# Down projections of a decoder block as seven-product quads in the pipeline of gate and up

## The chip, the cores and the metric

One core of a Trainium2 chip runs the whole block as one program. The metric is the device time of one execution in microseconds (us). TensorE (PE, with its weight loads PEld), VectorE (DVE), ScalarE (ACT), GpSimd (POOL) and SyncE (SP, which issues the transfers) work side by side, each through its own instructions in a fixed order.

## What is computed

The input is x, 2048 tokens by 1024 features, all in float32.

```python
xn = rmsnorm(h, g_mix); z = xn @ w_in + b_in           # 1024 -> 1536
y_conv = silu(layernorm(causal_depthwise_conv(a * sigmoid(gate))))   # 512 features, 31 taps
y_pool = (trailing mean over 2, 4, 8 or 16 tokens minus the token) @ w_pool * s_pool
h = h + concat(y_conv, y_pool) @ w_out
h = h + (silu(n @ w_gate) * (n @ w_up)) @ w_down        # n = rmsnorm(h, g_ffn); 1024 -> 2816 -> 1024
out = rmsnorm(h, g_final)
```

## The kernel before

The tokens are cut into two superblocks of 1024 (`a0`, `a1`), and each superblock into two halves of 512 tokens, which is the width of a matmul. Features lie on the partitions in blocks of 128. A product in float32 is made of three matmuls: every operand is split into a high and a low part (`split`, lines 195 and 196: ScalarE casts the high part, VectorE subtracts it to get the low part), and `mm3` (lines 204 to 206) adds high by high, high by low and low by high. So each operand that comes from memory costs a cast and a subtraction before TensorE can use it.

The order of the work, in the words of the program's end (from `a0, a1 = Sup(0), Sup(1)`): the input projection of superblock 0, then that of superblock 1 with superblock 0's convolution on VectorE beside it. Then for superblock 0 the output projection and `turn` (the norm and the start of gate and up), gate and up, and the down projection; then the same for superblock 1. Superblock 1's pooling and convolution (`bg`, some 160 steps, most of them one VectorE operation of 128x1024 in line 491) are spread by `beside` over superblock 0's gate and up, one step for each yield, and over its first two down groups.

**Gate and up** use seven products in place of eight (Strassen's scheme in a form that chains sums in PSUM). A `Quad` makes two output blocks for two halves of tokens from two blocks of weights. Its seven factors of the activations (`self.t`, made by `put_t`) stay in SBUF for the whole stage. Its weights are loaded two quads ahead (`load`, lines 851 and 852), summed (`sums`, lines 864 to 867) and split. `product` writes the banks of a two-bank accumulator (`quad`) and of one bank of `chain`; ScalarE copies banks on (lines 911, 916, 918), and VectorE and ScalarE form the results (lines 879 to 884). The seventh product's result is read from the accumulator's second bank before the third product adds to that bank. A gate quad and an up quad share one tile `at`, which is stored to `at_d`.

**Down** runs in three groups of 8, 8 and 6 blocks of the 22 (`GROUPS`). `down_load` (line 738) loads and splits the group's activations, `down` makes for each of eight output blocks a plain product into `pd`, and line 761 adds it to h, which is loaded from and stored to `h_d` (lines 756 and 765). The last group of superblock 1 is `down_last`.

Storage is given out by an `Arena`: 17 units for staging (`arena`), 36 for split operands (`arena_r`). `take` gives, in program order, the units that have been free longest; a tile of 1 MB takes two units. What the next user of a unit does must wait until the one before has been read. The order in which each engine runs its instructions is then set by a scheduler that keeps to dependences and prefers what comes first in the program.

## Time and profile before

| | |
|---|---|
| median of 3 runs (lowest to highest) | 1903.79 us (1899.77 to 1904.42) |
| profiled execution, its own time | 1902.86 us |
| span of its trace | 1901.1 us |
| mean granted TensorE clock | 0.987 |
| busy: PE, DVE, ACT | 97%, 65%, 33% |
| matmuls in the trace | 7995 |
| transfers | 263.96 MB, mean 139 GB/s |

"Busy" is the time in which an engine had an instruction in it, as a share of the span. A matmul is listed with 0.39 us, but the next starts before it ends, so that the distance between starts, not the listed length, says how many fit in a stretch. The granted clock is that of TensorE: 1.00 is 2.4 GHz, 0.50 is 1.2 GHz. An idle time in brackets behind an instruction is what its engine waited before it, and what ended the wait.

### The profile page before, as it was taken

Reading aid. Unit: us, or ns where it says so; the run is one execution under the profiler, and the core shown is the slowest. Engines: PE = TensorE matmul, PEld = TensorE weight load, DVE = VectorE, ACT = ScalarE, POOL = GpSimd, SP = SyncE. Lnnn points to the kernel's source line nnn. Section 1 sums busy time; section 2 is a strip of 40 time slices with the busy share of each in tenths; the row PEclk is TensorE's granted clock in tenths of the full one; section 3 lists DMA queues with packets and bytes.
Section 4 is the critical chain, followed back from the end, with each engine's and each line's share of the span. In section 5 each row is a group of like instructions: output and inputs, shape, how many; then the busy total and the mean of one; then the engine's idle time right before and its main releaser. Section 6 shows DMA issues by size and latency. Waiting matters only on the chain.

```text
span 1901.1 us, 19811 instructions
## 1 busy us (share of the span) xinstructions
PE 1841.0 (97%) x7995; PEld 1497.5 (79%) x7995; DVE 1234.7 (65%) x1359; ACT 623.2 (33%) x796; POOL 51.4 (3%) x41
## 2 busy tenths in 40 slices
PE   8999999998999999998999999899999999999996
PEld 6777887876788888877788888678888888888885
DVE  4989997488997999992542546866554545523235
ACT  5255124244333333341221323433333333412110
POOL 0103200000000000000000000000000000000000
PEclk9999999999999999998999999899999999999998
DMA  7263125523422232143583753155131113635422
GB/s 284 75 212 123 67 90 172 205 78 122 167 79 88 73 116 78 67 188 133 190 313 130 285 199 111 47 198 199 45 132 67 67 67 147 252 144 215 154 85 89
DMA packets 70235, 263.96 MB, mean 139 GB/s; under 512 B 7168, under 2 KB 11392, under 8 KB 56320
## 3 DMA queue, kind: packets, MB, share of 16 engines
q1 hardware_dynamic: 68848, 260.52, 38.1%
q10 hardware_dynamic: 1296, 2.19, 0.3%
q8 instruction: 62, 1.02, 0.2%
q14 instruction: 29, 0.24, 0.0%
HBM read 189.19 MB, written 73.49 MB: 138 GB/s over the span
## 4 chain that ended last, share of the span: by engine, by line
PE 83%; DVE 8%; DMA 4%; ACT 1%; issue 1%; POOL 0%; POOLq 0%; DVEq 0%; SPq 0%; ACTq 0%
PE pd L206 8%; PE pd L204 8%; PE pd L205 8%; PE quad L204 8%; PE quad L206 8%; PE quad L205 8%; PE chain L204 6%; PE chain L205 6%; PE chain L206 6%; PE px L204 3%; PE px L205 3%; PE px L206 3%; DVE arena_r L196 2%; DVE arena L491 2%; PE pa L206 1%
## 5 line engine op out<-in xcount | busy, mean ns | idle before, releaser
L195 ACT CAST arena_r<-arena 128x1024 fp32r<-128x1024 f32 (+3 forms) x375 | 364.4, 984 | 848.1 <-PE pd L205 228.9
L196 DVE TENSOR_TENSOR arena_r<-arena,arena_r 128x1024 fp32r<-128x1024 f32 (+3 forms) x375 | 422.2, 1138 | 246.5 <-ACT arena_r L195 215.5
L491 DVE SCALAR_TENSOR_TENSOR arena<-arena,par_sb 128x1024 f32<-128x1024 f32 (+1 forms) x240 | 287.2, 1212 | 2.3
L204 PE MATMUL quad<-arena_r 128*128 128x512 f32 x704 | 276.2, 393 | 11.7 <-ACT arena_r L195 10.8
L204 PE MATMUL pd<-arena_r 128*128 128x512 f32 x704 | 276.1, 392 | 9.9 <-ACT arena_r L195 9.1
L205 PE MATMUL quad<-arena_r 128*128 128x512 f32 x704 | 276.2, 392 | 0.8 <-DVE arena_r L196 0.8
L206 PE MATMUL pd<-arena_r 128*128 128x512 f32 x704 | 275.1, 391 | 1.8 <-DVE arena_r L196 1.8
L206 PE MATMUL quad<-arena_r 128*128 128x512 f32 x704 | 275.8, 392 | 0.0
L205 PE MATMUL pd<-arena_r 128*128 128x512 f32 x704 | 274.6, 390 | 0.0
L204 PE MATMUL chain<-arena_r 128*128 128x512 f32 x528 | 212.1, 402 | 4.9 <-ACT arena L916 2.8
L205 PE MATMUL chain<-arena_r 128*128 128x512 f32 x528 | 207.1, 392 | 0.9 <-DVE arena_r L196 0.9
L206 PE MATMUL chain<-arena_r 128*128 128x512 f32 x528 | 207.1, 392 | 0.0
L761 DVE TENSOR_TENSOR arena<-pd,arena 128x1024 f32<-128x1024 f32 x40 | 48.9, 1223 | 187.8 <-PE pd L206 186.7
L204 PEld LDWEIGHTS quad<-arena_r 128*128 128x128 f32 x704 | 133.3, 190 | 41.7 <-ACT arena_r L195 12.1
L204 PEld LDWEIGHTS pd<-arena_r 128*128 128x128 f32 x704 | 132.7, 188 | 39.1 <-ACT arena_r L195 10.2
L206 PEld LDWEIGHTS pd<-arena_r 128*128 128x128 f32 x704 | 132.5, 188 | 31.4 <-DVE arena_r L196 4.0
L205 PEld LDWEIGHTS quad<-arena_r 128*128 128x128 f32 x704 | 133.2, 189 | 29.3 <-DVE arena_r L196 1.9
L206 PEld LDWEIGHTS quad<-arena_r 128*128 128x128 f32 x704 | 133.3, 189 | 28.2 <-DVE arena_r L196 0.4
L205 PEld LDWEIGHTS pd<-arena_r 128*128 128x128 f32 x704 | 132.6, 188 | 27.9 <-issue 0.5
L204 PEld LDWEIGHTS chain<-arena_r 128*128 128x128 f32 x528 | 99.6, 189 | 38.0 <-ACT chain L911 8.8
L205 PEld LDWEIGHTS chain<-arena_r 128*128 128x128 f32 x528 | 99.9, 189 | 21.8 <-DVE arena_r L196 2.2
L206 PEld LDWEIGHTS chain<-arena_r 128*128 128x128 f32 x528 | 99.7, 189 | 21.8
(135 smaller groups left out, 2082.8 us busy)
## 6 DMA issues: line engine op xcount, KB each, us to landing
arena<-h_d SPq DMA_DIRECT2D x28, 1024.0 KB, 5.6
arena<-in_wg SPq DMA_DIRECT2D x44, 512.0 KB, 5.1
arena<-in_wu SPq DMA_DIRECT2D x44, 512.0 KB, 5.1
at_d<-arena SPq DMA_DIRECT2D x22, 1024.0 KB, 4.4
arena<-at_d SPq DMA_DIRECT2D x22, 1024.0 KB, 5.7
h_d<-arena SPq DMA_DIRECT2D x20, 1024.0 KB, 4.3
arena<-in_wd SPq DMA_DIRECT2D x32, 512.0 KB, 4.4
arena<-in_x SPq DMA_DIRECT2D x12, 1024.0 KB, 6.4
```

Source lines behind the costliest of these rows:

```text
L195: nc.scalar.copy(hi, y)
L196: tt(out=lo, in0=y, in1=hi.bitcast(F32), op=ALU.subtract)
L204: nc.tensor.matmul(acc, lhsT=w[:, 0, c], rhs=hi, start=start, stop=False, **kw)
L205: nc.tensor.matmul(acc, lhsT=w[:, 0, c], rhs=lo, start=False, stop=False, **kw)
L206: nc.tensor.matmul(acc, lhsT=w[:, 1, c], rhs=hi, start=False, stop=stop, **kw)
L491: stt(out=v, in0=u.ap[:, j : j + n], scalar=w, in1=v, op0=ALU.mult, op1=ALU.add)
L761: tt(out=v, in0=acc, in1=v, op=ALU.add)
```

## The change

Groups 0 and 1 of the down projection become quads too (`DownQuad`, four for each group), behind the 22 gate and up quads in the same pipeline. Their seven factors are formed while up quads end (`close`: four more VectorE subtractions for each up quad, stored to `t_d`), and loaded and split by `factors`, one for each product of the last quad ahead of a group. The quad adds its results to h (`open` loads it, `close` stores it). Group 2 stays as it was, with its loads stepped beside the last down quad (`follow`). `beside` now spreads `bg` over all quads, six steps for seven yields in place of one for one. In `turn`, the second norm's row sums go to a bank of the first quad's accumulator (`s.bank`) and stand ahead of three of the first four products; at the front, `x_spread` stands ahead of the second input tile.

```diff
+    t_d = [[dr.tile([P, 7, 4, T], F32, name=f"t_d{s}_{g}", bufs=1) for g in range(STRASSEN)] for s in range(NS)]
...
 
-        def __init__(self, src, halves=False, parts=None):
+        def __init__(self, src, halves=False, parts=None, pairs=None):
+            self.place = (lambda k: (k % pairs, k // pairs)) if pairs else (lambda k: (k // 2, k % 2))
             n = src.shape[1] // 2 if parts is None else T
             st = Buf(arena, 2 * n)
             v = st.ap.rearrange("p (a n) -> p a n", a=2)
...
                 ww, c = self(k)
-                r = mov[k // 2].v
+                i, h = self.place(k)
+                r = mov[i].v
                 for b, acc in accs:
-                    mm3(acc, ww, c, (r[:, 0, k % 2, b], r[:, 1, k % 2, b]), n == 0, n == len(ks) - 1)
+                    mm3(acc, ww, c, (r[:, 0, h, b], r[:, 1, h, b]), n == 0, n == len(ks) - 1)
 
         def free(self):
             self.w.free()
...
             self.t = {}
-            at = None
-            quads = []
-            for n in range(2 * NFP):
-                quads.append(Quad(self, n))
+            quads = [Quad(self, n) for n in range(2 * NFP)]
+            self.td = [{} for _ in range(STRASSEN)]
+            for g in range(STRASSEN):
+                quads[-1].follow = self.factors(g)
+                quads += [DownQuad(self, g, q, len(quads) + q) for q in range(NQ)]
+            quads[-1].follow = self.follow = self.down_load(STRASSEN)
             q0, q1 = quads[:2]
             q0.load()
             q1.load()
...
             q1.sums()
-            yield
-            for q in (q0, q1):
-                q.product(1)
-                q.product(2)
+            q0.begin()
+            q1.begin()
+            self.bank = q0.acc[:, 1]
+            yield
+            q0.product(1)
+            yield
+            q0.product(2)
+            yield
+            q1.product(1)
+            q1.product(2)
             q1.mid()
             yield
             yield from self.put_t(5, *B11, B12, B11)
...
-            for n in range(2, 2 * NFP):
+            for n in range(2, len(quads) - 2):
...
                 cur.product(3)
                 yield
 
+        def factors(self, g):
+
+            for p, i in ((1, 0), (2, 2), (6, 5), (5, 1), (7, 4), (4, 6), (3, 3)):
+                t = B4("tl")
+                nc.sync.dma_start(t.ap, t_d[self.s][g][:, i].rearrange("p n t -> p (n t)"))
+                self.td[g][p] = r = R("td")
+                for j in range(2):
+                    split(r.v[:, 0, j], r.v[:, 1, j], t.v[:, j])
+                t.free()
+                yield
+
         def down_load(self, g):
-            a = []
+            self.a = a = []
             for fp in range(*GROUPS[g]):
                 t = B4("al")
                 nc.sync.dma_start(t.ap, at_d[self.s][fp])
...
+
+        def open(self):
+            if self.gate:
+                Quad.at = B4("at")
+            self.at = Quad.at
+            self.o = self.at.v
+
+        def close(self):
+            if self.gate:
+                return
+            g, j = divmod(self.fp, 4)
+            if g < STRASSEN:
+                o = self.o
+                tx = B4("tx")
+                for dst, i0, i1 in (
+                    (tx.v[:, 0, 0], o[:, 1, 1], o[:, 0, 1]),
+                    (o[:, 0, 1], o[:, 0, 1], o[:, 0, 0]),
+                    (tx.v[:, 0, 1], o[:, 1, 1], o[:, 0, 1]),
+                    (tx.v[:, 1, 0], o[:, 1, 0], tx.v[:, 0, 1]),
+                ):
+                    tt(out=dst, in0=i0, in1=i1, op=ALU.subtract)
+                nc.sync.dma_start(t_d[self.sup.s][g][:, :4, j], self.at.ap.rearrange("p (n t) -> p n t", n=4))
+                nc.sync.dma_start(t_d[self.sup.s][g][:, 4:, j], tx.ap[:, : 3 * T].rearrange("p (n t) -> p n t", n=3))
+                tx.free()
+            else:
+                nc.sync.dma_start(at_d[self.sup.s][self.fp], self.at.ap)
+            self.at.free()
...
+        def begin(self):
+            if self.acc is None:
+                self.acc = ps2("quad")
+
-                self.acc = ps2("quad")
-                if self.gate:
-                    Quad.at = B4("at")
-                self.at = Quad.at
-                self.o = self.at.v
+                self.begin()
+                self.open()
-            r = self.sup.t[p].v
+            r = self.t[p].v
...
-            if self.n == 2 * NFP - 1:
-                self.sup.t.pop(p).free()
+            if self.follow:
+                self.t.pop(p).free()
+                step(self.follow)
...
-                if not self.gate:
-                    nc.sync.dma_start(at_d[self.sup.s][self.fp], self.at.ap)
-                    self.at.free()
+                self.close()
+
+    class DownQuad(Quad):
+
+
+        def __init__(self, sup, g, q, n):
+            self.sup, self.q = sup, q
+            self.s1, self.s2 = wd[g][2 * q], wd[g][2 * q + 1]
+            self.w = {}
+            self.ch = chain_bank[n % 2]
+            self.t = sup.td[g]
+            self.follow = None
+
+        def open(self):
+            self.h = B4("h")
+            nc.sync.dma_start(self.h.ap, h_d[self.sup.s][self.q])
+
+        def close(self):
+            nc.sync.dma_start(h_d[self.sup.s][self.q], self.h.ap)
+            self.h.free()
+
+        def result(self, a, b, acc, extra=None):
+            dst = self.h.v[:, a, b]
+            if extra is not None:
+                tt(out=dst, in0=dst, in1=extra, op=ALU.add)
+            tt(out=dst, in0=acc, in1=dst, op=ALU.add)
...
     wb.free()
     run(sq)
-    pa1 = a0.in_tile(in0.get(), "pa")
+    w = in0.get()
     a0.x_spread()
+    pa1 = a0.in_tile(w, "pa")
     a0.in_evac(0, pa, pg)
     cv = a0.mix_branches()
     pg1 = a0.in_tile(in0.get(), "pg")
...
                 step(gu, 2)
             elif n == 6:
                 step(gu)
-        nm = s.norm(1, s.hr)
+        nm = s.norm(1, s.hr, s.bank)
         step(gu)
-        step(nm, 2)
+        step(nm)
         step(gu)
+        step(nm)
+        step(gu, 2)
         step(nm)
         step(gu, 2)
         step(nm)
...
     g0 = a0.gate_up()
     turn(a0, g0)
     bg = seq(a1.pools(), a1.mix_branches())
-    beside(g0, bg, 6, 6)
-    beside(a0.down(0, a0.down_load(0)), bg, 3, 1)
-    beside(a0.down(1, a0.down_load(1)), bg, 4, 1)
+    beside(g0, bg, 6, 7)
     run(bg)
-    dn = a0.down(2, a0.down_load(2))
+    run(a0.follow)
+    dn = a0.down(STRASSEN)
     step(dn, 2)
     run(a1.y_load((2, 3, 0, 1)))
     step(dn, 4)
...
-    for g in range(len(GROUPS) - 1):
-        run(a1.down(g, a1.down_load(g)))
-    run(a1.down_last(len(GROUPS) - 1, a1.down_load(len(GROUPS) - 1)))
+    run(a1.follow)
+    run(a1.down_last(len(GROUPS) - 1))
```

The order of the instructions moves in three places that matter. The first is ScalarE near the program's start. `arena<-chain` is the copy of the norm's spread that the first evacuation needs. Before:

```order
L390 ACTIVATE arena,xss<-arena 128x1024 x4
L195 CAST arena_r<-arena 128x1024 x2
L199 ACTIVATE arena_r<-arena,par_sb 128x128 x4
L195 CAST arena_r<-arena 128x1024 x2
L399 COPY arena<-chain 128x1024
```

In the changed kernel:

```order
L393 ACTIVATE arena,xss<-arena 128x1024 x4
L197 CAST arena_r<-arena 128x1024 x3
L201 ACTIVATE arena_r<-arena,par_sb 128x128
L402 COPY arena<-chain 128x1024
L201 ACTIVATE arena_r<-arena,par_sb 128x128 x3
L197 CAST arena_r<-arena 128x1024
```

The copy has moved ahead of a cast and of three scaled casts; on TensorE the matmul that it waits for now stands 46 matmuls earlier.

The second is VectorE in superblock 0's turn. `px` is the output projection, `rv` the row scales of the second norm, `rb` their spread, L884 (L938 in the changed kernel) the result of the first up quad's second product. Before:

```order
L615 TENSOR_TENSOR arena<-px,arena 128x512
L196 TENSOR_TENSOR arena_r<-arena,arena_r 128x1024
L299 TENSOR_TENSOR arena<-arena 128x512
L323 TENSOR_SCALAR rv<-pv 128x4
L330 CAST rs<-rr 128x4
L331 TENSOR_TENSOR rs<-rr,rs 128x4
L334 TENSOR_TENSOR arena_r<-ident,rs 128x512 x2
L884 TENSOR_TENSOR arena<-quad,arena 128x512
L634 SCALAR_TENSOR_TENSOR arena<-arena,par_sb,rb 128x512 x3
L647 TENSOR_TENSOR arena<-arena 128x2x512
```

In the changed kernel:

```order
L618 TENSOR_TENSOR arena<-px,arena 128x512
L303 TENSOR_TENSOR arena<-arena 128x512
L326 TENSOR_SCALAR rv<-quad 128x4
L333 CAST rs<-rr 128x4
L334 TENSOR_TENSOR rs<-rr,rs 128x4
L337 TENSOR_TENSOR arena_r<-ident,rs 128x512 x2
L637 SCALAR_TENSOR_TENSOR arena<-arena,par_sb,rb 128x512 x2
L198 TENSOR_TENSOR arena_r<-arena,arena_r 128x1024
L650 TENSOR_TENSOR arena<-arena 128x2x512
L637 SCALAR_TENSOR_TENSOR arena<-arena,par_sb,rb 128x512 x2
L198 TENSOR_TENSOR arena_r<-arena,arena_r 128x1024
L938 TENSOR_TENSOR arena<-quad,arena 128x512
```

The norm no longer stands behind the result of the up quad, which shows that the products it belongs to now come after the norm's row sums.

The third is VectorE where superblock 0's first group of the down projection ends. Before, this is `down` (L761 adds a finished product to h) with the layer norm (L546, L309) beside it:

```order
L761 TENSOR_TENSOR arena<-pd,arena 128x1024
L196 TENSOR_TENSOR arena_r<-arena,arena_r 128x1024
L761 TENSOR_TENSOR arena<-pd,arena 128x1024
L196 TENSOR_TENSOR arena_r<-arena,arena_r 128x1024 x3
L761 TENSOR_TENSOR arena<-pd,arena 128x1024
L546 TENSOR_TENSOR arena<-arena,mu 128x1024 x3
```

In the changed kernel it is the fourth down quad, with the splits of the second factor set (L198), convolution steps (L494) and weight sums (L891, L892) between its results (L1005, L1006):

```order
L1006 TENSOR_TENSOR arena<-quad,arena 128x512 x2
L494 SCALAR_TENSOR_TENSOR arena<-arena,par_sb 128x1024
L198 TENSOR_TENSOR arena_r<-arena,arena_r 128x1024 x3
L494 SCALAR_TENSOR_TENSOR arena<-arena,par_sb 128x1024
L198 TENSOR_TENSOR arena_r<-arena,arena_r 128x1024 x2
L198 TENSOR_TENSOR arena_r<-arena,arena_r 128x512
L494 SCALAR_TENSOR_TENSOR arena<-arena,par_sb 128x1024
L891 TENSOR_TENSOR arena<-arena 128x512
L1005 TENSOR_TENSOR arena<-arena 128x512
L892 TENSOR_TENSOR arena<-arena 128x512
L198 TENSOR_TENSOR arena_r<-arena,arena_r 128x1024 x2
```

Six convolution steps or so stand in each down quad, where before the convolution was over by the start of the down projection; the factor splits come on top of them.

## Rows read from the trace of the kernel before

**Rows 1.** The page: busy time by engine, and the chain of waits by engine.

```profile
PE 1841.0 (97%) x7995; PEld 1497.5 (79%) x7995; DVE 1234.7 (65%) x1359; ACT 623.2 (33%) x796; POOL 51.4 (3%) x41
...
PE 83%; DVE 8%; DMA 4%; ACT 1%; issue 1%; POOL 0%; POOLq 0%; DVEq 0%; SPq 0%; ACTq 0%
```

**Rows 2.** Stage windows: stretch and length; PE, PEld, DVE, ACT, POOL busy (count); clock, DMA, GB/s.

```profile
946.50:1110.00 163.50, 163.50 (x722) 135.23 (x721) 70.00 (x62) 44.48 (x45) 0.00 (x0) 1.00 0.67 244
1268.50:1635.00 366.50, 366.50 (x1607) 299.89 (x1606) 194.58 (x237) 133.04 (x178) 0.00 (x0) 1.00 0.31 114
```

**Rows 3.** Stage windows at superblock 0's change from gate and up to down.

```profile
851.00:856.00 5.00, 0.94 (x5) 0.44 (x3) 3.65 (x4) 1.99 (x2) 0.00 (x0) 0.89 0.41 156
856.00:861.00 5.00, 0.33 (x1) 0.33 (x2) 0.35 (x1) 1.04 (x1) 0.00 (x0) 0.50 0.86 261
861.00:866.00 5.00, 4.96 (x13) 3.42 (x13) 0.88 (x1) 0.43 (x1) 0.00 (x0) 0.59 0.57 213
```

**Rows 4.** Timeline of PE, superblock 0's down: start, length, instruction, [wait before it].

```profile
860.67 0.80 PE L204 MATMUL pd<-arena_r 128*128 128x512 f32 x1 [8.73 <-ACT arena_r L195]
...
919.84 0.50 PE L204 MATMUL pd<-arena_r 128*128 128x512 f32 x1 [0.41 <-ACT arena_r L195]
921.88 0.50 PE L206 MATMUL pd<-arena_r 128*128 128x512 f32 x1 [1.30 <-DVE arena_r L196]
```

**Rows 5.** Stage windows: gate and up of superblock 0, then of superblock 1.

```profile
451.00:832.00 381.00, 380.11 (x1665) 310.29 (x1664) 349.64 (x382) 133.07 (x182) 0.00 (x0) 1.00 0.29 103
1255.00:1636.00 381.00, 381.00 (x1677) 311.62 (x1675) 204.67 (x250) 138.40 (x185) 2.48 (x1) 1.00 0.32 116
```

**Rows 6.** Timeline of DVE in superblock 0's gate and up.

```profile
647.50 0.68 DVE L865 TENSOR_TENSOR arena<-arena 128x512 f32<-128x512 f32 x1
648.11 1.28 DVE L491 SCALAR_TENSOR_TENSOR arena<-arena,par_sb 128x1024 f32<-128x1024 f32 x1
649.30 0.68 DVE L866 TENSOR_TENSOR arena<-arena 128x512 f32<-128x512 f32 x1
...
842.27 3.49 DVE L196 TENSOR_TENSOR arena_r<-arena,arena_r 128x1024 fp32r<-128x1024 f32 x3
```

**Rows 7.** Timelines of SP, ACT and DVE: one load of the down projection's activations, split.

```profile
845.79 0.32 SPq L738 DMA_DIRECT2D arena<-at_d  x1
...
851.04 1.99 ACT L195 CAST arena_r<-arena 128x1024 fp32r<-128x1024 f32 x2 [4.89 <-DMA arena<-at_d]
...
853.31 2.35 DVE L196 TENSOR_TENSOR arena_r<-arena,arena_r 128x1024 fp32r<-128x1024 f32 x2
```

**Rows 8.** The page's DMA issues, then instructions of `at_d`, loads and stores together.

```profile
arena<-at_d SPq DMA_DIRECT2D x22, 1024.0 KB, 5.7
...
DMA to landing us min/median/max: 4.2/5.0/8.7
```

**Rows 9.** Groups by line and shape: busy us, mean ns of one, idle before.

```profile
L918 ACT COPY arena<-chain 128x512 f32<-128x512 f32 x44 | 25.9, 588 | 79.4 <-PE chain L206 79.4
```

**Rows 10.** Timelines of DVE and PE in superblock 0's turn, then a stage window.

```profile
417.73 0.68 DVE L299 TENSOR_TENSOR arena<-arena 128x512 f32<-128x512 f32 x1
...
421.26 0.95 PE L316 MATMUL pv<-ones,arena 128*128 128x1 f32 x8
...
430.20 1.22 PE L204 MATMUL quad<-arena_r 128*128 128x512 f32 x2 [4.49 <-ACT arena_r L195]
...
430.00:435.00 5.00, 4.64 (x10) 3.25 (x11) 5.00 (x6) 1.20 (x2) 0.00 (x0) 0.50 0.00 0
```

**Rows 11.** Timeline of PE at the front, then two stage windows.

```profile
48.35 0.40 PE L346 MATMUL chain<-arena_r,ones_r 128*128 128x512 f32 x1
...
51.91 0.47 PE L204 MATMUL pg<-arena_r 128*128 128x512 f32 x1 [3.16 <-DVE arena L411]
...
40.00:50.00 10.00, 8.75 (x39) 6.89 (x37) 0.60 (x1) 1.68 (x2) 0.17 (x1) 1.00 0.12 45
50.00:60.00 10.00, 8.09 (x29) 6.52 (x30) 9.86 (x9) 3.66 (x4) 0.21 (x1) 0.83 0.30 105
```

More of the change, by code (lines that the diff above doesn't have):

```diff
@@ L185, in block_kernel @@
     class W(Buf):
[L188 removed]
+        WHERE = (range(7 * RU, NR), range(NR))
         def __init__(self, units, n=T):
@@ L550, in ln @@
             yield
-            var.rows(1.0 / CC, LN_EPS, chain if first else None)
+            var.rows(1.0 / CC, LN_EPS, flat(chain) if first else None)
             yield
@@ L625, in mix_out, with norm @@
                     r.free()
-        def norm(self, b, hr):
-            hr.rows(1.0 / D, RMS_EPS)
+        def norm(self, b, hr, bank=None):
+            hr.rows(1.0 / D, RMS_EPS, bank)
             yield
@@ L742, in down_load, with down @@
                 t.free()
-            return a
-        def down(self, g, a):
+                yield
+            self.ws = Ahead([lambda m=m: Dense(wd[g][m], pairs=GROUPS[g][1] - GROUPS[g][0]) for m in range(KD)], 1)
+            self.ws.prime(2)
+            yield
+        def down(self, g):
+            a, ws = self.a, self.ws
             n = len(a)
@@ L749, in down @@
                 self.fr = Rms(whole=True)
-            ws = Ahead([lambda m=m: Dense(wd[g][m]) for m in range(KD)], 1)
-            ws.prime(2)
             for m in range(KD):
```

15 lines of the change are left out of this document (9 added, 6 removed).

## The prediction

> **What bounds the kernel now.** I read the busy times and the chain of waits first: TensorE is busy 97% of the span and carries 83% of the chain that ends last [rows 1]. So I counted matmuls. One is listed as lasting 0.39 us, but each starts before the one ahead has ended; its price is the interval. The stage windows give it: 721 weight loads in 163.5 us of down projection, 0.2268 us each, and 1606 in 366.5 us of gate and up, 0.2282 us each, both at full clock [rows 2]. Then I looked for places where TensorE runs short of that pace. Four matter here: the front, the change from output projection to gate and up ("turn") of each superblock, and, in superblock 0 alone, the change from gate and up to down. Last I read VectorE by stage. In superblock 0's gate and up, with the convolution of superblock 1 beside it, VectorE is busy 349.6 of 381 us (92%); in superblock 1's, 204.7 of 381 us (54%) [rows 5]. That difference decides most of what follows.
>
> **Matmuls removed.** Groups 0 and 1 of a superblock's down projection were 2 x 8 output tiles x 8 blocks x 2 halves x 3 passes = 768 matmuls. As eight quads of 7 products x 4 blocks x 3 passes they are 672. 768 x 0.2268 = 174.2 us; 672 x 0.2282 = 153.4 us; so 20.8 us less per superblock on the engine that sets the end.
>
> **Superblock 1.** Nothing runs beside it, and the order of instructions puts the factor loads and splits a quad (84 x 0.2282 = 19.2 us) ahead of their use. VectorE spends 1.14 us on a 1024-wide subtraction, 0.61 us on a 512-wide one and 1.20 us on a convolution step, by the distance between starts [rows 6]. A down quad gives it 3 wide and 11 narrow operations: 10.1 us. The 14 wide splits of a factor set add 16 us, spread over two quads, so no quad passes 19.2 us by much. I take 20 us; the ends are 21 (nothing waits) and 15 (two or three waits of 2 us for each factor set, like the small waits of [rows 4]).
>
> **Superblock 0, what leaves.** At the change to down, TensorE waits 8.73 us for the first weights and then runs at half clock, 0.50 and 0.59 of full [rows 3, 4]. In those 15 us it does 5+1+13 = 19 matmuls; at pace there would be 66, so 10.7 us are lost. Down quads now follow up quads in one pipeline, with weights fetched two quads ahead, so this goes. A later wait of 1.3 us at the layer norm and 0.4 us before it go as well. With the matmuls that is 20.8 + 10.7 + 1.7 = 33.2 us to be had.
>
> **Superblock 0, what comes.** First, VectorE. In the new order, from the last up quad's seventh product to the sixth down quad's, it has 46 wide subtractions, 67 narrow operations and 29 convolution steps: 52.4 + 40.9 + 34.8 = 128.1 us. TensorE needs six quads, 115.2 us, and about 1.9 us for four layer-norm matmuls: 117.1 us. VectorE falls 11 us behind. Its result of the seventh product must be read before the third product may write the same bank; two products (24 x 0.2282 = 5.5 us) lie between, less one copy on ScalarE (0.59 us [rows 9]) and two narrow operations (1.2 us). So 3.7 us are cover and 7.3 us become waiting.
>
> Second, the staging of factors. Working the arena's rule through in program order, five of the seven loads of the first set, and six of the second, take one and the same pair of units, since the convolution holds most others. Such a load can start only when the one before is split. The trace shows one such link: load issued at 845.79, two casts from 851.04, two subtractions from 853.31 [rows 7]. Priced apart: 5.7 us for 1 MB [rows 8], 2.0 us of casts, 1.2 us for the last subtraction, 8.9 us together. Counting from the end of the first product of the quad that steps the loads (the first load is in by then), the second set's five links finish at 3.2 + 5 x 8.9 = 47.7 us; its last factor is wanted 15 products later, at 15 x 12 x 0.2282 = 41.1 us. So it is 6.6 us late. The first set, with four links, is ready at 40.9 us, just in time. 7.3 + 6.6 = 13.9; I take 14 us. Ends: if loads land as fast as the quickest (4.2 us) and the reserve holds, 7; if as slowly as the slowest (8.7 us), the second chain is 3.0 x 5 = 15 us later and no cover is left for the 11 us, 33 us. A wait of ScalarE's cast for such a load also holds back the bank copies queued behind it, and TensorE waits for those; this lies within the same ends.
>
> For the load the trace has 4.2 to 8.7 us for 1 MB, with 5.7 in the median [rows 8], in company with weights. The Trainium skill (SBUF — State Buffer, "The DMA setup-cost knee") fits 2 us plus bytes over 436 GB/s, an estimate of 4.4 us here. By that the links would be 1.3 us shorter, the last factor 0.1 us late, and the sum 6.5 us better.
>
> So superblock 0 gives 33.2 - 14 = 19 us (0 to 26).
>
> **Turns.** The second norm's row sums now stand ahead of 24 first-pair products instead of behind them, in a bank of the quad's own accumulator. TensorE got to them at 421.26, while what they sum was ready at 417.73 + 0.68 = 418.4 [rows 10]. So the norm starts 2.9 us sooner, and the 24 moved products (5.5 us) cover the 4.49 us wait after it. I take 3 us per turn, 6 in all. At most the wait and the half-clock stretch go whole, 4.5 + 2.6 us each; at least nothing, as VectorE's chain of sums and splits behind it is no shorter. I use 0 to 11 for both.
>
> **Front.** The spread of x's norm is moved ahead of the second input tile. Its fourth matmul had stood behind that tile, at 48.35; the evacuation of the first pair followed, and the next tile waited 3.16 us for a bank and began at reduced clock [rows 11]. From 40 to 60 us there are 39 + 29 = 68 matmuls where 20 / 0.2268 = 88 fit: 4.6 us. All of it should go: the fourth needs nothing that the three ahead of the tile did not have. Ends 2 (a later wait takes some back) and 6.
>
> **Costed at nothing:** the four extra subtractions per up quad (2.4 us in 38.4) displace one convolution step in seven (one of seven yields per quad, 2.4 us per pair), so VectorE stays at about 92%; the extra stores and loads of factors, some 25 MB, fall on DMA engines that are busy 29 to 32% in those stages [rows 5]. If that cover went, they would show as late loads, priced above.
>
> **Sum.** 4.6 + 6 + 19 + 20 = 49.6 us off the profiled execution's 1902.9 us: 1853 us. The median of the runs shown is 0.9 us above that execution, which I leave out.
>
> **The rivals.** (a) The stalls are hidden: loads land like the quickest [rows 8], convolution steps slip behind the quads' own work, and less than 7 us of waiting is left in superblock 0. For it: most loads have a quad of slack. Against: one pair of units, and a VectorE that is full in every link. 1853 - 14 = 1839 us with none left, 1833 with the best ends of turns and front, 1842 in the middle. (b) VectorE and staging eat superblock 0's gain: stalls near 33 us, 19 us more than forecast, 1872 us. For it: in-order queues, where one late load stops results behind it. (c) Slower than before: every factor load of superblock 0 lands on the path, 14 x 8.9 = 125 us against 63.8 us (33.2 + 20 + 6 + 4.6) gained elsewhere, 1964 us. It decides from the eighth exposed load on. Against it: the first loads of each set find free units well ahead. (d) Stalls cancel the whole gain, near 1903 us: the same mechanism with seven loads exposed.
>
> **How the numbers follow.** Forecast 0.57 (1846 to 1862), (a) 0.19, (b) 0.17, (c) 0.04, (d) 0.03. About 0.3%, 6 us, can be told from no change. Faster 0.94, same 0.02, slower 0.04. The range, 1835 to 1875 us, holds the forecast, most of (a) and (b), and leaves out the rest.
>
> **What would show it.** Matmuls fewer by 192; no wait of 8 us near 850 us; 20 us less between superblock 1's last up quad and its third group; in superblock 0's down quads VectorE near full and TensorE waiting on results of the seventh product and on casts behind factor loads; the 3.16 us wait at 52 us gone. It is wrong if those quads run at TensorE's pace in superblock 0, if superblock 1's do not, or if gate and up of superblock 0 slow down.

## The result and the profile after

The change takes 1876.1 us, the median of 4 runs (1874.1 to 1878.4), where the kernel before takes 1904.1. The ratio is 0.985, with a 95% interval of 0.983 to 0.988. So 28 us were gained where 50 were forecast, and the time lies 1 us above the range. The profiled execution spans 1874.5 us.

The page of the change, busy times and chain by engine, against [rows 1]:

```profile
PE 1806.9 (96%) x7803; PEld 1462.6 (78%) x7803; DVE 1390.5 (74%) x1607; ACT 698.6 (37%) x900; POOL 54.6 (3%) x41
...
PE 81%; DVE 10%; DMA 3%; ACT 2%; issue 2%; POOL 0%; SPq 0%; POOLq 0%; DVEq 0%; ACTq 0%
```

The 192 matmuls are gone and PE is 34 us less busy, but the span fell by 26.6 us only: TensorE now waits more than it did. To see where, I put the same marks into both traces. "Lost" is what the intervals between starts of matmuls exceed 0.2282 us, added up where an interval is over 0.25.

| stage | before, us (lost) | change, us (lost) | gained | forecast |
|---|---|---|---|---|
| front, to the first matmul of output projection 0 | 324.3 (25.1) | 316.9 (17.8) | 7.4 | 4.6 |
| turn 0, first three quads | 78.0 (13.7) | 81.1 (16.7) | -3.1 | 3 |
| gate and up 0, 18 quads | 346.3 (2.7) | 345.3 (2.2) | 1.0 | 0 |
| last up quad to output projection 1 | 278.4 (16.5) | 273.8 (33.2) | 4.6 | 19 |
| turn 1, first three quads | 83.8 (17.1) | 85.4 (18.4) | -1.6 | 3 |
| last up quad of superblock 1 to the end | 278.9 (7.9) | 260.7 (10.4) | 18.2 | 20 |

Superblock 1 went as forecast. In superblock 0 nearly all the time that the matmuls saved was lost again. Its row splits in two: 19.6 us are lost from the last up quad to the third group, and 13.6 us in the third group itself, which the prediction had not looked at. Stage windows of the change (columns as in [rows 2]): gate and up 0, last up quad to third group, third group, last up quad of superblock 1 to its third group.

```profile
481.22:826.56 345.34, 345.25 (x1514) 282.24 (x1512) 307.72 (x351) 121.17 (x164) 0.00 (x0) 1.00 0.34 119
826.56:1022.92 196.36, 186.10 (x789) 147.56 (x788) 179.06 (x200) 87.23 (x103) 2.49 (x1) 0.98 0.63 224
1022.92:1100.35 77.43, 67.62 (x283) 54.45 (x281) 34.95 (x31) 23.68 (x25) 0.00 (x0) 0.93 0.75 268
...
1613.76:1791.56 177.80, 175.27 (x767) 142.99 (x766) 130.55 (x155) 82.36 (x98) 0.00 (x0) 1.00 0.66 242
```

VectorE is busy 91% of the second row and 73% of the fourth: the same quads, with and without background work. Smaller windows show it at 94 to 99% where the down quads run:

```profile
855.00:875.00 20.00, 16.93 (x67) 13.19 (x66) 18.76 (x22) 5.81 (x8) 0.00 (x0) 0.91 0.78 263
875.00:895.00 20.00, 19.29 (x85) 15.68 (x84) 19.76 (x24) 6.03 (x8) 0.00 (x0) 1.00 0.41 158
...
940.00:965.00 25.00, 20.84 (x76) 15.37 (x77) 23.89 (x28) 8.14 (x10) 0.00 (x0) 0.93 0.72 251
```

The wait of 8.73 us at the change to down [rows 4] is gone. The longest now stands in the third group (timeline of PE, waits alone):

```profile
1047.52 0.50 PE L206 MATMUL pd<-arena_r 128*128 128x512 f32 x1 [1.55 <-ACT arena_r L197]
...
1049.29 0.50 PE L208 MATMUL pd<-arena_r 128*128 128x512 f32 x1 [1.03 <-DVE arena_r L198]
...
1064.51 0.80 PE L206 MATMUL pd<-arena_r 128*128 128x512 f32 x1 [7.23 <-ACT arena_r L197]
```

What is late there are the group's weights. Timeline of SP's queue over this stretch:

```profile
999.28 0.32 SPq L563 DMA_DIRECT2D y_d<-arena  x1
1001.89 0.33 SPq L227 DMA_DIRECT2D arena<-in_wd  x1
...
1022.21 0.33 SPq L227 DMA_DIRECT2D arena<-in_wd  x1
...
1027.15 0.32 SPq L472 DMA_DIRECT2D arena<-y_d  x1
...
1036.43 0.32 SPq L472 DMA_DIRECT2D arena<-y_d  x1
...
1041.51 0.32 SPq L472 DMA_DIRECT2D arena<-y_d  x1
1042.95 0.33 SPq L227 DMA_DIRECT2D arena<-in_wd  x1
1043.49 5.22 SPq L472 DMA_DIRECT2D arena<-y_d  x3
```

For 20.7 us, from 1022.21 to 1042.95, no weight load is issued, though a tile of 36 matmuls takes 8.2 us. In front of it in the queue stand loads of superblock 1's y, each held until its buffer is free and all behind it held too: the y load of 1027.15 is released by the split of the weights loaded at 1022.21, that of 1036.43 by the split of that y, and the weight load of 1042.95 by the split of this second y. It is the buffers that are late, not y's data: `y_load` takes the pooled half of y first, and that was stored by 517. But the buffers are late because the background work is. The group's first weights go where convolved y stood: the load of 1001.89 is issued when the y store of 999.28 has landed, the second one behind the last y store, and the third at 1022.21. So the first y load comes 4.2 us behind the group's start (1022.92) and the next weight load 20.0 us behind it. In the kernel before, the last y was stored 52 us sooner, the first y load came 9.9 us ahead of the group's start (1044.83), the next weight load 3.3 us behind it. Instructions of `y_d`, stores of convolved y alone, of before and then of the change:

```profile
L560 SPq DMA_DIRECT2D y_d<-arena x4: 319/323/327, 950.6 to 954.6; - x4
```

```profile
L563 SPq DMA_DIRECT2D y_d<-arena x4: 319/320/423, 999.3 to 1006.5; - x4
```

Theory A: superblock 0 loses to the background work, which runs beside the down quads (VectorE) and ends too late (the third group). Its rivals come with the runs.

### The profile page after: what moved, and what is told of

Its sections match the earlier page's. It is cut to its first block, busy times and chain, and to the rows that moved or that the text cites. A ratio compares the mean times of both kernels' runs of the same rounds, so it can differ in the third digit from the quotient of the medians.

```text
span 1874.5 us, 19934 instructions
## 1 busy us (share of the span) xinstructions
PE 1806.9 (96%) x7803; PEld 1462.6 (78%) x7803; DVE 1390.5 (74%) x1607; ACT 698.6 (37%) x900; POOL 54.6 (3%) x41
## 4 chain that ended last, share of the span: by engine, by line
PE 81%; DVE 10%; DMA 3%; ACT 2%; issue 2%; POOL 0%; SPq 0%; POOLq 0%; DVEq 0%; ACTq 0%
PE quad L206 11%; PE quad L207 10%; PE quad L208 10%; PE chain L206 9%; PE chain L207 8%; PE chain L208 8%; DVE arena_r L198 4%; PE px L206 3%; PE px L208 3%; PE px L207 3%; PE pd L206 2%; PE pd L208 2%; PE pd L207 2%; DVE arena L494 2%; PE pa L207 1%
## 5 line engine op out<-in xcount | busy, mean ns | idle before, releaser
L197 ACT CAST arena_r<-arena 128x1024 fp32r<-128x1024 f32 (+2 forms) x431 | 414.2, 976 | 707.2 <-PE quad L207 191.8
L198 DVE TENSOR_TENSOR arena_r<-arena,arena_r 128x1024 fp32r<-128x1024 f32 (+2 forms) x431 | 480.0, 1130 | 192.2 <-ACT arena_r L197 187.0
L206 PE MATMUL quad<-arena_r 128*128 128x512 f32 x960 | 376.8, 393 | 5.4 <-DVE arena L1006 2.2
L207 PE MATMUL quad<-arena_r 128*128 128x512 f32 x960 | 375.6, 391 | 2.4 <-DVE arena_r L198 2.4
L208 PE MATMUL quad<-arena_r 128*128 128x512 f32 x960 | 375.6, 391 | 0.0
L206 PE MATMUL chain<-arena_r 128*128 128x512 f32 x720 | 289.8, 403 | 15.1 <-ACT arena L972 6.8
L494 DVE SCALAR_TENSOR_TENSOR arena<-arena,par_sb 128x1024 f32<-128x1024 f32 (+1 forms) x240 | 287.5, 1214 | 2.3
L207 PE MATMUL chain<-arena_r 128*128 128x512 f32 x720 | 283.9, 394 | 5.2 <-DVE arena_r L198 5.2
L208 PE MATMUL chain<-arena_r 128*128 128x512 f32 x720 | 283.1, 393 | 0.0
L206 PEld LDWEIGHTS quad<-arena_r 128*128 128x128 f32 x960 | 181.0, 189 | 47.9 <-DVE arena L1006 4.2
L207 PEld LDWEIGHTS quad<-arena_r 128*128 128x128 f32 x960 | 181.2, 189 | 41.1 <-DVE arena_r L198 3.6
L208 PEld LDWEIGHTS quad<-arena_r 128*128 128x128 f32 x960 | 181.2, 189 | 37.9
L206 PEld LDWEIGHTS chain<-arena_r 128*128 128x128 f32 x720 | 136.4, 189 | 63.9 <-ACT chain L967 22.3
L207 PEld LDWEIGHTS chain<-arena_r 128*128 128x128 f32 x720 | 136.9, 190 | 33.6 <-DVE arena_r L198 6.9
L208 PEld LDWEIGHTS chain<-arena_r 128*128 128x128 f32 x720 | 136.9, 190 | 29.2
L206 PE MATMUL px<-arena_r 128*128 128x512 f32 x256 | 100.0, 392 | 0.0
L208 PE MATMUL px<-arena_r 128*128 128x512 f32 x256 | 99.7, 389 | 0.0
L207 PE MATMUL px<-arena_r 128*128 128x512 f32 x256 | 99.7, 389 | 0.0
L933 DVE TENSOR_TENSOR arena<-quad,arena 128x512 f32<-128x512 f32 x88 | 60.4, 687 | 34.7 <-ACT arena L974 30.0
L206 PE MATMUL pd<-arena_r 128*128 128x512 f32 x192 | 76.7, 399 | 9.6 <-ACT arena_r L197 8.8
L208 PE MATMUL pd<-arena_r 128*128 128x512 f32 x192 | 76.0, 396 | 1.0 <-DVE arena_r L198 1.0
L207 PE MATMUL pd<-arena_r 128*128 128x512 f32 x192 | 75.7, 394 | 0.0
```

The lines of the kernel that those rows point to most:

```text
L197: nc.scalar.copy(hi, y)
L198: tt(out=lo, in0=y, in1=hi.bitcast(F32), op=ALU.subtract)
L206: nc.tensor.matmul(acc, lhsT=w[:, 0, c], rhs=hi, start=start, stop=False, **kw)
L207: nc.tensor.matmul(acc, lhsT=w[:, 0, c], rhs=lo, start=False, stop=False, **kw)
L208: nc.tensor.matmul(acc, lhsT=w[:, 1, c], rhs=hi, start=False, stop=stop, **kw)
L494: stt(out=v, in0=u.ap[:, j : j + n], scalar=w, in1=v, op0=ALU.mult, op1=ALU.add)
```

## The experiments

Each is the change with the edit shown, unless said. All times are medians, with the ratio to the kernel before on the same chip. Stages are those of the table and come from the one profiled execution of each run.

**1. Superblock 1 alone.** `STRASSEN` becomes a pair, one number for each superblock:

```diff
-STRASSEN = 2
+STRASSEN = (0, 2)
...
-    beside(g0, bg, 6, 7)
-    run(bg)
-    run(a0.follow)
+    beside(g0, bg, 6, 6)
+    run(a0.down_load(0))
+    beside(a0.down(0), bg, 3, 1)
+    run(a0.down_load(1))
+    beside(a0.down(1), bg, 4, 1)
+    run(bg)
+    run(a0.down_load(2))
```

> Superblock 0 goes back to plain down projections for its first two groups, with the background work spread over them as before; superblock 1 keeps the down quads; front and turns stay as in the change. Theory A (superblock 0's down quads save 33 us and lose almost all of it again, 15 us beside the quads and 14 us in its third group, so that they are worth about 4.5 us): about 1880 us. Rival (superblock 0's down quads are worth the forecast 19 us and what is missing went elsewhere): about 1895 us.

1883.2 us, 0.988 (0.986 to 0.990). The last up quad to output projection 1 takes 278.2 us, as before the change. Superblock 0's down quads are worth 4.4 us there. Theory A's 4.5 us hold for the stage; the whole kernel is 3 us above its 1880. The rival's 19 us and 1895 us are refuted.

**2. The old turn.** The row sums stand behind the first-pair products, in their own bank:

```diff
-        nm = s.norm(1, s.hr, s.bank)
+        nm = s.norm(1, s.hr)
         step(gu)
-        step(nm)
+        step(nm, 2)
         step(gu)
-        step(nm)
-        step(gu, 2)
```

(in `gate_up`, products 1 and 2 of both quads again behind one `yield`)

> The change with the turns' order of before alone: the second norm's row sums behind the first-pair products, in a bank of their own. Theory A (asking for the row sums before they are ready made the first three quads 3.1 and 1.5 us longer): 4.6 us less than the change, about 1871.5 us, with the first three quads back at 78.0 and 83.8 us. Rival (the order of the turn costs nothing; its longer time comes from what else is in the kernel): 1876 us.

1874.6 us, 0.984 (0.982 to 0.985). The turns take 81.2 and 84.7 us: turn 0 did not come back. The expectation failed; something besides the order makes the turn longer. Runs 5 and 6 look for it.

**3. y spread over the third group.**

```diff
-    step(dn, 2)
-    run(a1.y_load((2, 3, 0, 1)))
-    step(dn, 4)
+    yl = a1.y_load((2, 3, 0, 1))
+    step(dn)
+    for _ in range(5):
+        step(dn)
+        step(yl, 2)
```

> The change, with superblock 1's y loaded two blocks at a time between the tiles of superblock 0's third down group instead of all eight blocks behind its second tile. Theory A (y's loads and casts stand in the queues ahead of the group's weights and casts, and that makes its 280 matmuls last 77.4 us instead of 63.5): the group takes at most 67 us and the kernel about 1864 us. Rival (the DMA engines are full there, and the same bytes in another order wait as long): 76 us or more for the group, 1876 us in all.

1871.3 us, 0.982 (0.980 to 0.983). The group takes 71.1 us and loses 7.4 instead of 13.6: between the two expectations. The y loads matter, but spreading them is not enough.

**4. A light convolution.**

```diff
-                else:
+                elif not self.s:
                     stt(out=v, in0=u.ap[:, j : j + n], scalar=w, in1=v, op0=ALU.mult, op1=ALU.add)
```

> The change without 30 of the 31 taps of superblock 1's depthwise convolution on VectorE (left out, so its result is another); loads, buffers and the order of all else stay. VectorE has some 35 us less to do beside superblock 0's down quads. Theory A (half of the 15 us of stalls there is VectorE being late, half the chain of factor loads on one pair of buffers): stalls of 6 to 8 us are left in those eight quads. Rival 1 (all of it is VectorE): 2 us or less. Rival 2 (all of it is the chain): 13 us or more.

1865.8 us, 0.979 (0.977 to 0.980). The down stretch loses 8.7 us instead of 19.6 with VectorE at 79% of it; superblock 1's loses 3.9.

```profile
829.20:1013.71 184.51, 180.33 (x784) 144.62 (x783) 145.39 (x170) 87.50 (x104) 1.95 (x1) 1.00 0.65 244
```

So 10.9 us were VectorE's lateness, and what is left is just above theory A's 6 to 8. The third group still loses 11.8 us. There the order of the program counts, not VectorE's load: y is stored 11 us sooner than in the change, but the group starts 9 us sooner too (1013.71), and the weight load behind the first y loads again comes 19.9 us behind its start.

```profile
L563 SPq DMA_DIRECT2D y_d<-arena x4: 319/320/320, 990.0 to 995.6; - x4
```

Whether the remaining 8.7 us are the chain of factor loads is left to run 13.

**5 and 6. The old reserve**, with the new turn and then with the old one as well. The change has one line more than its diff above shows: in `W`, the split weights may lie from the seventh slot of moving operands on, where they began at the eighth. This puts the line back:

```diff
-        WHERE = (range(7 * RU, NR), range(NR))
+        WHERE = (range(8 * RU, NR), range(7 * RU, NR), range(NR))
```

> The change with one line put back: the arena again keeps eight slots of moving operands apart from the weights and asks for seven only after that. The turns' new order stays. Theory B (it was this line that made the turns longer: with it VectorE makes three subtractions and then three splits where the change alternates them, and TensorE's granted clock does not fall a second time): the first three quads take 77 to 79 us and 82.5 to 84 us, the kernel some 4 us less than the change. Rival (what the new order of row sums costs is the loss, whatever the reserve): 81 and 85 us, no difference.

> As the run before it, and the turns' old order too. Theory B: the first three quads take 78.0 and 83.8 us as in the kernel before, 4.6 us less than the change in all. Rival (the turn is longer because of what the new pipeline puts behind it): 81 and 85 us.

Run 5: 1876.9 us, 0.986 (0.985 to 0.987); turns 83.1 and 86.3 us. Run 6: 1871.6 us, 0.983 (0.982 to 0.984); turns 77.9 and 85.6 us. A turn's time alone can mislead, because the granted clock differs between executions: runs 3 and 10 have the change's turn 0, matmul for matmul and with the same waits, and take 82.1 and 79.6 us. So here are TensorE's waits, added up, and the mean granted clock beside it:

| | turn 0, us | waits | clock | turn 1, us | waits | clock |
|---|---|---|---|---|---|---|
| before | 78.0 | 8.5 | 0.96 | 83.8 | 8.0 | 0.92 |
| change | 81.1 | 9.4 | 0.94 | 85.4 | 10.1 | 0.94 |
| run 2, old order | 81.2 | 9.1 | 0.92 | 84.7 | 10.0 | 0.92 |
| run 5, old reserve | 83.1 | 9.9 | 0.92 | 86.3 | 10.6 | 0.94 |
| run 6, both | 77.9 | 8.2 | 0.96 | 85.6 | 8.1 | 0.90 |

Theory B holds only in both halves together: old order and old reserve give the waits back in both turns, either alone does not. In run 6 turn 1 stays long because TensorE ran longer at the lower level, not because it waited more. Windows of turn 0 (PE's count and the granted clock, third from the right, are what to look at), first of the kernel before, then of run 2, which has the old order and the new reserve:

```profile
430.00:435.00 5.00, 4.64 (x10) 3.25 (x11) 5.00 (x6) 1.20 (x2) 0.00 (x0) 0.50 0.00 0
...
440.00:445.00 5.00, 3.13 (x11) 1.53 (x9) 4.93 (x6) 3.99 (x5) 0.00 (x0) 1.00 0.43 164
445.00:450.00 5.00, 3.59 (x15) 2.47 (x14) 5.00 (x6) 4.85 (x6) 0.00 (x0) 1.00 0.11 20
```

```profile
424.00:429.00 5.00, 3.92 (x10) 2.81 (x11) 5.00 (x6) 1.43 (x2) 0.00 (x0) 0.61 0.00 0
...
434.00:439.00 5.00, 2.83 (x11) 1.80 (x10) 5.00 (x5) 2.10 (x2) 0.00 (x0) 0.98 0.92 333
439.00:444.00 5.00, 3.81 (x10) 2.50 (x9) 4.75 (x6) 4.53 (x6) 0.00 (x0) 0.50 0.15 61
```

VectorE is full in both. In the kernel before, TensorE drops to the lower of its two levels once. In run 2 it drops again after further waits and does 10 matmuls in 5 us where the other does 15. The change has that second drop too (0.50 from 437.5 to 442.5). What the reserve moves is the order of VectorE's work. Timeline of DVE, of the kernel before and of run 2:

```profile
439.10 3.49 DVE L647 TENSOR_TENSOR arena<-arena 128x1024 f32<-128x1024 f32 x3
442.50 3.64 DVE L196 TENSOR_TENSOR arena_r<-arena,arena_r 128x1024 fp32r<-128x1024 f32 x3
```

```profile
433.33 1.21 DVE L650 TENSOR_TENSOR arena<-arena 128x1024 f32<-128x1024 f32 x1
434.46 1.22 DVE L198 TENSOR_TENSOR arena_r<-arena,arena_r 128x1024 fp32r<-128x1024 f32 x1
435.60 1.21 DVE L650 TENSOR_TENSOR arena<-arena 128x1024 f32<-128x1024 f32 x1
```

Three subtractions and then three splits before, one of each in turn after. That this order brings the second drop is argued from these rows, not shown by itself.

**7. Short factor loads.**

```diff
-                nc.sync.dma_start(t.ap, t_d[self.s][g][:, i].rearrange("p n t -> p (n t)"))
+                nc.sync.dma_start(t.ap[:, :T], t_d[self.s][g][:, i, 0])
```

> The change with a quarter of each down factor fetched (256 KB of 1 MB; the rest of the buffer is what stood there, so the result is another); casts and subtractions stay whole. A link of the chain of factor loads is some 2 to 3 us shorter. Theory A (the chain on one pair of buffers makes about half of what superblock 0's down quads lose, VectorE the rest, and they add): the stretch from the last up quad to the third group loses 5 to 8 us less than the change's 19.6. Rival 1 (VectorE sets the links, the transfers are cover): under 2 us less. Rival 2 (nearly all is the transfers): over 12 us less.

1876.7 us, 0.986 (0.984 to 0.987). The down stretch loses 21.3 us, no less than the change's 19.6. That is rival 1's number, but not its reason: the links did become shorter. The last three loads of the second set, in the change and then here (x2 in 10.32 or 7.93 us, and so the distance of two starts):

```profile
932.07 10.32 SPq L749 DMA_DIRECT2D arena<-t_d  x2
...
952.01 0.33 SPq L749 DMA_DIRECT2D arena<-t_d  x1
```

```profile
930.21 7.93 SPq L749 DMA_DIRECT2D arena<-t_d  x2
```

A link takes 10.0 us in the change and 7.6 or less here, and the last load is issued at 937.8 instead of 952.0. TensorE gains nothing from it, so the chain's loads are not what it waits for.

**8. y behind the third group.**

```diff
-    step(dn, 2)
-    run(a1.y_load((2, 3, 0, 1)))
-    step(dn, 4)
+    step(dn, 6)
     a1.mix_weights()
     run(dn)
+    run(a1.y_load((2, 3, 0, 1)))
```

> The change with superblock 1's y loaded behind superblock 0's third group. Theory A (y's loads on one pair of buffers, in SyncE's queue ahead of the group's weights, make that group lose 13.6 us): the group loses 3 us or less, and the output projection behind it pays part of that, as y is late there. Rival (the loads of h and of x, 1 MB each, that now start at once fill the DMA engines, and that alone holds the weights back): the group still loses 8 us or more.

1873.0 us, 0.984 (0.982 to 0.985). The two windows are the third group and the output projection behind it:

```profile
1021.80:1085.50 63.70, 63.70 (x283) 52.74 (x281) 27.67 (x25) 17.02 (x18) 0.00 (x0) 1.00 0.76 271
1085.50:1179.48 93.98, 88.44 (x371) 70.71 (x370) 55.17 (x60) 34.21 (x35) 1.01 (x1) 0.95 0.47 160
```

The group now runs at TensorE's pace and loses nothing, though the DMA share is as high as in the change (0.76 against 0.75). The rival is refuted: it was the y loads. The projection behind pays 11.0 us, since y is late for it, so the wait for the most part moved.

**9 and 14. The old front**, with the new reserve and then with the old one (the edit of run 5) too:

```diff
-    w = in0.get()
-    a0.x_spread()
-    pa1 = a0.in_tile(w, "pa")
+    pa1 = a0.in_tile(in0.get(), "pa")
+    a0.x_spread()
```

> The change with the spread of x's norm back behind the second input tile. Theory C (the front's 7.4 us come from two edits: this move, 4.6 us as the count of missing matmuls said, and the smaller reserve for moving operands, about 3 us, since the two runs with the old reserve begin the output projection 3 to 4.5 us later than the change): the output projection begins at about 321.5 us. Rival (the move alone gives it): at about 324.

> The change with both the spread of x's norm back behind the second tile and the reserve of eight slots. Theory C (the move gives 3.1 us of the front's 7.4 and the reserve the other 4): the output projection begins at 323.5 to 324.5 us, as in the kernel before. Rival (the reserve has no part in it, and the front differs by 3 us from one run to the next): 319 to 321 us.

Run 9: 1878.0 us, 0.986 (0.985 to 0.987), output projection from 320.0. Run 14: 1881.9 us, 0.988 (0.987 to 0.990), from 323.9, as before the change (324.3). The ends alone prove little: thirteen kernels here, the change among them, have the same instructions in the front, and theirs lies between 316.3 and 319.8, with a clock of 0.97 to 1.00 between 100 and 200 us. The change, run 9 and run 14 all have 1.00 there, so they can be compared: the move gives 3.1 us, the reserve 3.9 more when the order is the old one. The matmuls say the same. From 40 to 60 us the change has 90, run 9 has 77 (3.0 us fewer), and run 14 has 68, as before the change.

```profile
40.00:50.00 10.00, 8.98 (x40) 7.08 (x38) 2.39 (x5) 2.19 (x4) 0.00 (x0) 1.00 0.15 48
50.00:60.00 10.00, 8.48 (x37) 7.05 (x38) 9.82 (x10) 2.46 (x3) 0.42 (x2) 1.00 0.31 102
```

With the new order the old reserve (run 5) leaves these windows full and costs 11 matmuls from 60 to 100 us, 2.5 us. So theory C's two edits account for the front, but the reserve's part depends on the order.

**10. More background work.**

```diff
-    beside(g0, bg, 6, 7)
+    beside(g0, bg, 6, 6)
```

> The change with a step of background work at every step of gate and up and of the down quads, where the change skips one in seven. Some 24 us of VectorE's convolution go from superblock 0's down quads to its gate and up, where VectorE has 37.6 us to spare. Theory D (superblock 0's down quads lose their time to VectorE alone, which is 94 to 97% busy there; the light convolution took 10.9 us off): the stretch from the last up quad to the third group loses 9 to 12 us where the change loses 19.6, gate and up loses at most 2 us more, the kernel takes about 1868 us. Rival (gate and up becomes longer by as much): 1876 us.

1857.0 us, 0.975 (0.974 to 0.977): 19 us less than the change, by one number. Third group, last up quad to third group, gate and up 0:

```profile
1014.50:1077.51 63.01, 63.01 (x280) 52.19 (x278) 33.14 (x30) 21.68 (x23) 0.00 (x0) 1.00 0.74 269
825.69:1014.50 188.81, 181.58 (x792) 146.18 (x791) 154.97 (x179) 88.62 (x105) 1.95 (x1) 1.00 0.70 259
480.13:825.69 345.56, 345.27 (x1514) 282.53 (x1512) 333.72 (x375) 121.16 (x165) 0.00 (x0) 1.00 0.32 114
```

Gate and up takes 26 us more of VectorE's work and is 0.2 us longer. The down stretch loses 11.4 us instead of 19.6, and the third group nothing at all instead of 13.6: y is stored from 913.5 on, the group's weights no longer wait for it, and the y loads start 8.4 us ahead of the group's start (1014.50) instead of 4.2 behind. The weight load behind them then comes 8.4 us after the start, not 20.0.

```profile
L563 SPq DMA_DIRECT2D y_d<-arena x4: 319/366/987, 913.5 to 920.6; - x4
```

```profile
1001.72 0.33 SPq L227 DMA_DIRECT2D arena<-in_wd  x1
...
1006.05 9.55 SPq L472 DMA_DIRECT2D arena<-y_d  x4
...
1017.69 1.84 SPq L472 DMA_DIRECT2D arena<-y_d  x2
1022.92 0.33 SPq L227 DMA_DIRECT2D arena<-in_wd  x1
```

Theory D had expected 1868, from the down stretch alone; the third group's 13.6 us came on top. This shows the cause of the third group's loss and of 8.2 of the down stretch's 19.6 us. Of the 11.4 that are left there, 3.9 occur in superblock 1 too; the other 7.5 are not explained.

**11, 12 and 16. Combinations.** Run 11 has the old turn, y spread, and the eight-slot reserve from the turn on; run 12 adds the edit of run 10; run 16 is run 10 with the old turn alone. The late reserve:

```diff
-            super().__init__(arena_r, 2 * units * n, self.WHERE)
+            super().__init__(arena_r, 2 * units * n, ((range(8 * RU, NR),) if arena.tidy else ()) + self.WHERE)
```

> The change with the old turn, with the old reserve from the turn on only, and with y's loads spread two by two over the third group. If the parts add: the turn of superblock 0 3.2 us shorter and the third group 5 to 6 us, the front as in the change: about 1867 us. If the turn's gain is lost to the layout again: 1871 us.

> The run before it with a step of background work at every step as well. If theory D is right and the parts add: 8 to 10 us less than the run before, about 1858 us, which would beat both kernels. Rival (more background in gate and up costs there what it saves behind): no less than the run before.

> Background work at every step, and the turns' old order. If the parts add as the old turn alone did (1.5 to 3 us): about 1854.5 us, with the second turn's first three quads back from 87.9 to about 84.7 us. Rival (the turn's time goes by the layout of buffers that each edit shifts): 1857 us.

Run 11: 1873.5 us, 0.984 (0.982 to 0.985). Run 12: 1861.8 us, 0.978 (0.976 to 0.980). Run 16: 1854.1 us, 0.975 (0.973 to 0.977). The turn's gain did not add: turn 0 takes 84.1 us in run 11 (an execution of 1877.8 us), 82.3 in run 12, 81.1 in run 16, and TensorE's waits in it are 13.2, 11.6 and 9.2 us, none below the change's 9.4 by more than 0.2. Run 16 came out at the 1854.5 that was expected, but not by the way named, and its interval takes in the rival's 1857. Run 16 and run 10 are the same within their intervals, and the fastest; both beat the change and the kernel before.

**13. Light convolution and short factors.** The edits of runs 4 and 7.

> The light convolution and the short factors together (30 of 31 taps left out, a quarter of each down factor fetched). With VectorE no longer full, the stretch from the last up quad to the third group lost 8.7 us where superblock 1's, with nothing beside it, loses 3.9. Theory A (the chain of factor loads on one pair of buffers is the rest, hidden behind VectorE until then): 3 us or more less than 8.7. Rival (the transfers never mattered; what is left is VectorE's own work for the layer norm, the factors and the results): within 1 us of 8.7.

1862.2 us, 0.978 (0.977 to 0.980). The down stretch loses 7.7 us; it lost 8.7 with whole factors. The rival holds: even with VectorE relieved, the transfers are worth no more than 1 us, by which runs with the same down stretch differ as well (runs 2 and 3 by 1.1). What makes up the rest over superblock 1's 3.9 wasn't taken apart.

**15. Still more background work.**

```diff
-    beside(g0, bg, 6, 7)
+    beside(g0, bg, 8, 7)
```

> The change with eight steps of background work in every seven, where the change makes six in seven and the fastest run so far seven in seven. Theory D (the sooner the background work is done, the less the down quads lose, as long as gate and up has VectorE to spare; it would have some 97% there now): the stretch that loses 11.4 us at seven in seven loses 6 to 9, gate and up loses 2 us or less more, about 1853 us. Rival (VectorE has reached its limit in gate and up, the loss moves there): 1857 us or more.

1857.7 us, 0.976 (0.975 to 0.978), no better than run 10. Gate and up takes 349.0 us and loses 5.0 instead of 2.1; the down stretch loses 11.0. VectorE is busy 342.7 of the 349.0 us (98%): it has reached its limit in gate and up, as the rival said.

## Why the prediction was right or wrong

**Matmuls removed and superblock 1** were right. The 192 matmuls left, and superblock 1 gained 18.2 us where 20 was forecast between 15 and 21. It loses 10.4 us to waits there, 2.5 more than before.

**Superblock 0, what leaves** was right: the 8.73 us wait and the half clock behind it are gone.

Of 49.6 us forecast 26.5 came in the two traces. Two parts failed: superblock 0's down projection gave 14.4 us too little (4.6 for 19), the turns 10.7; the rest nearly cancels.

**Superblock 0, what comes.** The step that failed is "Costed at nothing". I wrote that the four extra subtractions "displace one convolution step in seven" and that VectorE "stays at about 92%". Gate and up indeed did not suffer (VectorE 89%). But a displaced step is not gone: the background work ended some 50 us later than before, in the buffers that the third group's weights need, and the load of its result in that group was not in the sum at all. Run 10 undoes that displacement alone: the third group gets 13.6 us back and the down stretch 8.2, while gate and up is no longer than it was. It had room for the 26 us all along, though not for one step in seven more (run 15).

**The two terms for stalls**, 7.3 and 6.6 us, came to 14, and the down stretch lost 19.6, of which 3.9 also occur in superblock 1. That the other 15.7 lie near 14 is luck: the parts were not right. VectorE's lateness was 10.9 us (run 4), not 7.3. The second set's links were priced about right (8.9 us, 10.0 measured), but shortening them was worth nothing (run 7), and at most 1 us with VectorE relieved (run 13), where the term had 6.6. So the price of a load decided nothing. A factor load took 5.4 us in the median, near the 5.7 of [rows 8]. The 4.4 us estimated from the Trainium skill (SBUF — State Buffer, "The DMA setup-cost knee") was too short in this company. Two readings were wrong without harm: 4.2 and 8.7 us, the ends taken for the load, are both stores (the loads alone took 4.6 to 8.5 us), and four links make the first set ready at 38.8 us by the formula, not at 40.9.

**Turns**: forecast +6 us, measured -4.7. The step that failed is that the norm starts sooner and the moved products cover the wait behind it. The row sums do start 3 us sooner, and the 4.49 us wait is gone. But TensorE now waits 2.18 us for the row sums, as the moved products no longer stand there to cover it, and again further on:

```profile
410.82 1.05 PE L319 MATMUL quad<-ones,arena 128*128 128x1 f32 x8 [2.18 <-DVE arena L303]
...
436.12 0.80 PE L207 MATMUL chain<-arena_r 128*128 128x512 f32 x1 [1.82 <-DVE arena_r L198]
...
439.82 0.79 PE L206 MATMUL chain<-arena_r 128*128 128x512 f32 x1 [1.19 <-ACT arena L972]
```

So the waits grew, from 8.5 to 9.4 us and from 8.0 to 10.1, where 3 us less were forecast for each. Behind the row sums VectorE's chain of sums and splits is as long as it was, which the prediction had as its lower end (0). In turn 0 the clock falls a second time, which it had not. It had no negative end, and it passed over the line with the reserve. The order alone is not the cause: run 2 puts it back and gains nothing, run 6 needs both.

**Front**: forecast 4.6 us, measured 7.4. The move gave 3.1 (run 9); the same overlooked line gave the rest (runs 9 and 14). TensorE's two windows of [rows 11] are now full, so the mechanism was the one named.

```profile
40.00:50.00 10.00, 10.00 (x45) 8.23 (x44) 8.62 (x12) 1.74 (x2) 0.21 (x1) 1.00 0.36 133
50.00:60.00 10.00, 10.00 (x45) 8.29 (x45) 9.79 (x8) 0.63 (x1) 1.15 (x1) 1.00 0.01 2
```

Rival (b), 1872 us with stalls near 33 us, came nearest: 33.2 us were lost in superblock 0's down projection. Its words, "in-order queues, where one late load stops results behind it", describe the third group. But it placed them in the down quads and in the factor loads, so that its number fits is partly luck.

## What to carry to other kernels

When work off the critical path is slowed to make room, follow it to its end and ask who reads its result and who needs its buffers: here one step in seven, free where it was taken out, cost 22 us in the two stages behind. Before a chain of transfers is put into a sum, ask whether the engine that sets the time waits at its end: here the chain became shorter by 14 us and nothing was gained. A one-line change to where buffers lie can move as much time as the edit that one looks at: here 4 us at the front, and waits in the turn. And before a difference of 2 or 3 us in one stage is explained, look at the waits and the granted clock beside the time.

## What was not expected of the hardware

In run 2 TensorE's granted clock came back to the higher level at 432 and fell again at 439, after waits of only 0.34 and 1.82 us, and stayed low for 7 us. In the kernel before, waits of at most 1.39 us in the same products kept the higher level. Turn 0 took between 77.9 and 84.1 us over these kernels, with the same matmuls in all of them. A part of that is the clock alone. In the change, run 10 and run 3, TensorE has the same instructions in turn 0 and the same waits, 9.4 us, but the granted clock was 0.94, 0.96 and 0.92:

```profile
400.13:481.22 81.09, 71.72 (x288) 54.97 (x286) 64.41 (x80) 31.78 (x41) 1.01 (x1) 0.94 0.28 101
```

```profile
400.52:480.13 79.61, 70.23 (x287) 53.80 (x286) 65.92 (x81) 31.75 (x41) 1.01 (x1) 0.96 0.30 109
```

```profile
399.50:481.62 82.12, 72.75 (x287) 55.51 (x286) 64.51 (x80) 31.76 (x41) 1.01 (x1) 0.92 0.27 100
```

What makes the clock differ between executions of the same instructions is not shown.
